# Narrower context columns in three projections, and the norm of each tile issued behind its own output projection

## The chip, the cores and the metric

One core of one Trainium2 chip runs the whole program. The time is device microseconds (us) of one execution; lower is better. Shapes are partitions x elements. PE is the matrix engine, DVE the vector engine, ACT the scalar engine, POOL the general engine, SP the queue that issues most DMAs. Each engine works through its own list of instructions in order; an instruction that waits holds up all that stand behind it on that engine.

## The reference, cut to what matters

Two layers of a block with three token mixers (a gated linear attention "ml", a decayed linear attention "hg", a differential softmax attention "da") and a gated feed-forward network. The input has 256 latent tokens `x` and 256 context tokens `ctx`; only `x` is returned.

```python
for l in range(DEPTH):                       # DEPTH = 2
    with_ctx = l < DEPTH - 1                 # the last layer makes no context output
    pc = split_cols(hc @ w_in + b_in)        # context rows: keys and values are needed in both layers,
    px = split_cols(hx @ w_in + b_in)        # queries only where with_ctx
    ...
    yx = jnp.concatenate([mx, gx, ax], axis=-1) @ w_out
    x = x + gx1 * rmsnorm(yx, g_post_mix[l])
    hx = rmsnorm(x, g_pre_ffn[l]) * (1.0 + ax2) + sx2
    x = x + gx2 * rmsnorm(swiglu(hx, ...), g_post_ffn[l])
```

So in the second layer the query columns of the context rows, and the gate columns of the context rows, are used by nothing.

## The kernel before

Tokens are four tiles of 128 rows: tiles 0 and 1 are context, 2 and 3 are latent. `full` is true in the first layer and false in the second; `qt` are the tiles that need queries (all four, then 2 and 3), `halves` the halves that need an output.

A projection is `gemm_tm`. It takes 256 columns of a weight at a time. Each weight block (512 rows x 256 columns) is loaded as `wraw`, cast by ACT to `whi` (L297), and the rest `wraw - whi` is made by DVE as `wlo` (L298), both in the format fp32r; there are two buffers of each. For every tile and each of the 8 slices of the contraction, PE loads a 128x128 piece of the activation `hT` as weights and streams 128x256 of `whi` or `wlo` past it: two products with `whi` (activation high and low part) and one with `wlo`. All of them have line L302. One projection of one tile is thus 24 products of 256 columns, and of four tiles 96. A PSUM bank `mm` holds two tiles (0 and 1, or 2 and 3); `add_bias` (L913) or `ev_vo` (L1069, L1076) takes a bank out.

In the second layer the query, key and value columns of da and ml come in blocks of 256: `qk` (three blocks, q is 0 to 383, k is 384 to 767), then the rest of the da values, `ev_vo` (three blocks: 0 to 383 values, 384 to 767 gates), and `mqk` (three blocks, again q then k). Block 0 is made for tiles 2 and 3 alone. Block 1 straddles the border, and is made whole for all four tiles.

The order on every engine is made when the program is built: a scheduler places instructions by priority and by its own estimates of how long each takes, and uses the projections as filler between the dependent steps of the mixers. The two places of concern are these. While the last two heads of hg run in lockstep (`hg_mix`, L811 to L868, then `hg_out`, L880 to L886: ACT copies `Ck`, PE multiplies into `mx`, DVE updates `Kh` and `Qd`), PE is given the products of `qk` blocks 0 and 1 between those steps. While `da_tile` runs for tiles 2 and 3 (L982 scores, L984 maximum, L988 exponentials, L994 difference, L997 transposes, L999 copy, L1003 values), PE is given the products of `ev_vo` and the first of `mqk`. Behind each of these two blocks come stretches of projections alone: behind hg the rest up to the transposes of `pad` (L968) that open da, behind da the rest up to the transposes of `mqk` (L1100).

At the end of the mixers `out_rest` makes the output projection. In the second layer the last half of its columns is made tile by tile (tile 2, then tile 3), and behind each tile `ev_z` (L1175 product with the gate, L1177 squares) and `post_norm` (L471, L473 on POOL, L475 into `R`) are issued. After both, `norm_T` calls `norm_rows` for each tile (L426 squares of `R` on ACT, `rstd` L415 and L416 on POOL, L428 scaled rows `nsc` on DVE), then PE transposes `nsc` (L447, L455), and ACT and DVE make `hT` for the feed-forward network (L461 to L466).

Of the kernel before, what the change touches and what calls it, by code (L numbers as in the profile page):

```python
# [15 lines left out]
ALU = mybir.AluOpType  # L16
# [85 lines left out]
def dit_block(ctx: ExitStack, tc: tile.TileContext, x, c, ctx_in, c_ctx, w_ada, b_ada, g_pre_mix,  # L102
# [220 lines left out]

    def gemm_tm(srcs, act, tiles, evac, pre=None):

        n = sum(p.shape[-1] for p in srcs[0])
        tiles = list(tiles)
        wide = n > 256  # L330
        bank = lambda t: t if wide else t // 2
        banks = {b: pst([P, 512] if wide else [P, 2, 256], mm=True) for b in sorted({bank(t) for t in tiles})}
        dst = lambda t: banks[t][:, :n] if wide else banks[bank(t)][:, t % 2, :n]
        new = lambda t: wide or t - 1 not in tiles or t % 2 == 0
        for si, blk in enumerate(blocks_of(srcs)):
            end = si == len(srcs) - 1
            if pre is not None and end:
                pre()
            if wide and end:
                for t in tiles:  # L340
                    upper(dst(t), blk, act, t, si == 0)
                    lower(dst(t), blk, act, t, True)
                    evac([t], dst(t))
            else:

                for t in tiles:
                    upper(dst(t), blk, act, t, si == 0 and new(t))
                for t in tiles:
                    lower(dst(t), blk, act, t, end)
            ada_step()  # L350
        if not wide:
            for tb, b in banks.items():
                tt = [t for t in tiles if bank(t) == tb]
                evac(tt, b[:, tt[0] % 2:tt[-1] % 2 + 1, :n])
# [254 lines left out]
    for l in range(DEPTH):  # L609
# [301 lines left out]

        def add_bias(dst, w, nb, bb):
            return lambda tt, ps: V.tensor_tensor(dst[:, tt[0]:tt[-1] + 1, w:w + nb], ps[:, :, :nb],  # L913
                                                  bb.over(0, nb, len(tt)), op=ALU.add)

        qk = stg.tile([P, 4, 768], F32, tag="qk", name=nm("qk"))
        for i in range(3):
            bb = Bias([b_in[l, O_DAQ + i * 256:O_DAQ + (i + 1) * 256]])
            gemm_tm(w_src(w_in[l], O_DAQ + i * 256, 256), hact, qt if i == 0 else range(4), add_bias(qk, i * 256, 256, bb), pre=bb.load)
        bb = Bias([b_in[l, O_DAV:O_DAV + 256]])  # L920
# [138 lines left out]
        for i in range(3):  # L1059
            bb = Bias([b_in[l, O_MLV + i * 256:O_MLV + (i + 1) * 256]])  # L1060

            def ev_vo(tt, ps, i=i, bb=bb):
                c_ = 0
                while c_ < 256:
# [13 lines left out]
                    c_ += w  # L1078
            gemm_tm(w_src(w_in[l], O_MLV + i * 256, 256), hact, range(4) if i < 2 else qt, ev_vo, pre=bb.load)
        mqk = stg.tile([P, 4, 768], F32, tag="qk", name=nm("mqk"))  # L1080
        for i in range(3):
            bb = Bias([b_in[l, O_MLQ + i * 256:O_MLQ + (i + 1) * 256]])
            gemm_tm(w_src(w_in[l], O_MLQ + i * 256, 256), hact, qt if i == 0 else range(4), add_bias(mqk, i * 256, 256, bb), pre=bb.load)

# [75 lines left out]

        Z, zss = {}, {}

        zbank = {}
# [28 lines left out]
        def out_rest(hf):  # L1192
# [6 lines left out]
            for cb in range(4):  # L1199
                hi, lo = ws[cb] = wload([w_out[l, 0:512, cb * 256:(cb + 1) * 256]])  # L1200
                if full or cb < 2:
                    for t in tt_:
                        out_mm(t, cb, hi, 0, True, False, False)
                    for t in tt_:
                        out_mm(t, cb, lo, 0, False, False, True)
                        if cb % 2:
                            ev_z(t, cb // 2)
            if not full:

                for t in tt_:  # L1210
# [3 lines left out]
                    with tc.high_priority(offset=CHAIN):  # L1214
                        ev_z(t, 1)
                        post_norm(t, Z[t], zss[t])

        ada_flush()
# [33 lines left out]
        with tc.tile_pool(name=f"ff{l}", bufs=1, reuse_waits="tile") as ff:  # L1252
# [5 lines left out]
            for hf in halves:  # L1258
                scr = norm_scr(ff, "nsc")
                if full:  # L1260
# [3 lines left out]
                else:  # L1264
                    with tc.high_priority(offset=CHAIN):
                        norm_T(u1, s1_, hf, scr)
            Z = {t: yp.tile([P, D], F32, tag=f"Y{t}", name=nm("Z")) for t in qt}
# [107 lines left out]
```

## Time and profile before

| what | us |
|---|---|
| median of 3 runs (lowest, highest) | 1347.56 (1346.56, 1349.05) |
| profiled execution, its own time | 1347.59 |
| its span (first to last instruction on the trace) | 1345.9 |
| PE busy in it | 1284.2 (95%) |
| DVE, ACT, POOL busy | 898.6, 624.9, 202.3 |

The second layer starts at about 815 us of the span, its hg mixer ends near 976, da runs from 999 to 1058, the output projection ends at 1139 and the feed-forward network fills 1151 to 1335. A row of the timeline is: start us, duration us, engine, line, operation, result<-inputs, shapes, count, and in brackets the idle time ahead of it with what ended that. Several instructions of a kind in a row are one row; its duration runs to the end of the last. The duration of a matrix product includes its drain, so the spacing of products, and not their duration, tells what a stream of them costs.

### The profile page before, as it was taken

To read this page: it belongs to the slowest core of one execution; us is meant where nothing else is said; L and a number is where in the kernel's file an instruction comes from. 1 tells how busy PE (TensorE), PEld (TensorE's weight loads), DVE (VectorE), ACT (ScalarE), POOL (GpSimd) and SP (SyncE) were. 2 spreads that over 40 slices of the span, in tenths; PEclk is the share of its full clock that TensorE was granted. 3 is DMA by queue.
4 is the path that set the end of the run, shared out by engine and by line. 5 is a ranking of instruction groups with operands and counts; after the bars stand their busy time and mean duration, and the time that the engine had idled before them with its cause. 6 is when DMAs were issued, how large, how long until landed. Compare 5 with 4: busy or idle time off the path is not lost.

```text
span 1345.9 us, 23128 instructions
## 1 busy us (share of the span) xinstructions
PE 1284.2 (95%) x9022; PEld 1094.6 (81%) x9022; DVE 898.6 (67%) x1564; ACT 624.9 (46%) x1188; POOL 202.3 (15%) x304
## 2 busy tenths in 40 slices
PE   7998999999989899999999999899999998999997
PEld 5785889778888798778887888778897998788886
DVE  4899998554688998476336348566855456666666
ACT  3436352578354653212221236546536724554543
POOL 3133202111142300001000003133111202000001
PEclk9999999999989999999999999899999999899999
DMA  9772526132244677477335235532331313456563
GB/s 290 227 221 75 164 64 201 41 114 72 95 141 142 192 253 229 141 255 243 116 100 178 94 111 151 148 95 63 104 95 51 122 47 109 142 188 188 188 188 125
DMA packets 158443, 194.05 MB, mean 144 GB/s; under 512 B 10524, under 2 KB 132806, under 8 KB 158334
## 3 DMA queue, kind: packets, MB, share of 16 engines
q1 hardware_dynamic: 156910, 188.89, 44.9%
q0 software_dynamic: 1424, 3.68, 1.0%
q8 instruction: 71, 1.16, 0.3%
q14 instruction: 38, 0.31, 0.1%
HBM read 191.47 MB, written 1.08 MB: 143 GB/s over the span
## 4 chain that ended last, share of the span: by engine, by line
PE 76%; DVE 10%; ACT 5%; issue 4%; DMA 3%; POOL 3%; SPq 0%; DVEq 0%; POOLq 0%; ACTq 0%
PE mm L302 62%; DMA araw<-in_w_ada_dram 2%; PE mx L1126 2%; DVE wlo L298 2%; PE mx L982 2%; PE mx L1003 1%; DVE acc L228 1%; PE mm L1114 1%; ACT whi L297 1%; POOL rstd L416 1%; PE mx L997 1%; PE mm L164 1%; DVE accq L228 1%; PE mx L880 1%; PE ada L233 1%
## 5 line engine op out<-in xcount | busy, mean ns | idle before, releaser
L297 ACT CAST whi<-wraw 128x1024 fp32r<-128x1024 f32 (+1 forms) x247 | 256.4, 1039 | 415.7 <-PE mm L302 365.2
L298 DVE TENSOR_TENSOR wlo<-wraw,whi 128x1024 fp32r<-128x1024 f32 (+1 forms) x243 | 295.8, 1218 | 193.0 <-PE mm L302 94.4
L302 PE MATMUL mm<-hT,whi 128*128 128x512 f32 (+1 forms) x1568 | 352.0, 372 | 4.4 <-ACT hT L465 2.1
L302 PEld LDWEIGHTS mm<-hT,whi 128*128 128x128 f32 x1568 | 270.8, 189 | 55.7 <-issue 4.0
L302 PE MATMUL mm<-whi,hT 128*128 128x256 f32 (+1 forms) x1792 | 264.3, 293 | 3.1 <-ACT hT L1157 1.4
L302 PEld LDWEIGHTS mm<-whi,hT 128*128 128x128 f32 x1792 | 234.0, 192 | 19.2 <-issue 8.4
L302 PE MATMUL mm<-hT,wlo 128*128 128x256 f32 (+1 forms) x960 | 185.0, 334 | 0.0
L302 PEld LDWEIGHTS mm<-hT,wlo 128*128 128x128 f32 x960 | 152.9, 190 | 21.1 <-issue 0.4
L302 PE MATMUL mm<-wlo,hT 128*128 128x256 f32 (+1 forms) x896 | 140.8, 292 | 0.0
L302 PE MATMUL mm<-whi,GT 128*128 128x512 f32 x504 | 129.5, 397 | 0.0
L302 PEld LDWEIGHTS mm<-wlo,hT 128*128 128x128 f32 x896 | 119.1, 191 | 10.9 <-issue 10.4
L302 PEld LDWEIGHTS mm<-whi,GT 128*128 128x128 f32 x504 | 93.7, 188 | 24.5 <-ACT whi L297 1.6
L228 DVE SCALAR_TENSOR_TENSOR accq<-araw,csil,accq 128x1024 f32<-128x1024 f32 x63 | 81.2, 1295 | 29.8 <-DMA araw<-in_w_ada_dram 29.7
L302 PE MATMUL mm<-wlo,GT 128*128 128x512 f32 x252 | 70.0, 396 | 0.0
L228 DVE SCALAR_TENSOR_TENSOR acc<-araw,csil,acc 128x1024 f32<-128x1024 f32 x49 | 62.8, 1306 | 4.6 <-DMA araw<-in_w_ada_dram 4.4
L302 PEld LDWEIGHTS mm<-wlo,GT 128*128 128x128 f32 x252 | 47.3, 188 | 11.3
L415 POOL TENSOR_SCALAR rstd<-hss 128x1 f32<-128x1 f32 (+2 forms) x44 | 18.8, 427 | 241.7 <-ACT hsq L656 159.9
L1327 POOL TENSOR_TENSOR Z<-Z,gg 128x512 f32<-128x512 f32 x6 | 9.4, 1572 | 234.1 <-ACT sqz L1326 234.1
L988 ACT ACTIVATE e<-mx,damx 128x512 f32<-128x512 f32 (+1 forms) x48 | 29.3, 618 | 26.3 <-DVE damx L985 26.3
L811 ACT COPY Ck<-Kh 128x512 f32<-128x512 f32 (+1 forms) x56 | 28.8, 525 | 25.7 <-DVE Kh L836 18.9
L416 POOL TENSOR_TENSOR rstd<-rstd,mhalf 128x1 f32<-128x1 f32 (+2 forms) x58 | 40.0, 690 | 4.7
L984 DVE TENSOR_REDUCE damx<-mx 128x1 f32<-128x512 f32 (+1 forms) x48 | 28.3, 598 | 18.0 <-PE mx L982 17.1
(283 smaller groups left out, 1499.9 us busy)
## 6 DMA issues: line engine op xcount, KB each, us to landing
araw<-in_w_ada_dram SPq DMA_DIRECT2D x80, 512.0 KB
wraw<-in_w_in_dram SPq DMA_DIRECT2D x68, 512.0 KB
wraw<-in_w_ffn_down_dram SPq DMA_DIRECT2D x50, 512.0 KB
wraw<-in_w_ffn_gate_dram SPq DMA_DIRECT2D x48, 512.0 KB
wraw<-in_w_ffn_up_dram SPq DMA_DIRECT2D x48, 512.0 KB
wraw<-in_w_out_dram SPq DMA_DIRECT2D x24, 512.0 KB
aw<-in_w_ada_dram SPq DMA_DIRECT2D x16, 512.0 KB
wraw<-in_w_in_dram SPq DMA_DIRECT2D x12, 256.0 KB
```

Source lines behind the costliest of these rows:

```text
L164: PE.matmul(acc0[3][:, :P], lhsT=ident, rhs=ident, start=True, stop=True, skip_group_check=True)
L228: V.scalar_tensor_tensor(out=a, in0=raw, scalar=csil[:, k, r:r + 1], in1=a, op0=ALU.mult, op1=ALU.add)
L297: S.copy(hi[:, :nk, :n], raw[:, :nk, :n])
L298: (eng or V).tensor_tensor(lo[:, :nk, :n], raw[:, :nk, :n], hi[:, :nk, :n], op=ALU.subtract)
L302: PE.matmul(ps, lhsT=lhs, rhs=rhs, start=first, stop=last, skip_group_check=True)
L415: G.tensor_scalar(o[:, :width], ss, 1.0 / n, EPS, ALU.mult, ALU.add)
L416: G.tensor_tensor(o[:, :width], o[:, :width], mhalf[:, :width], op=ALU.pow)
L811: S.copy(C[:, q0:].rearrange("p (a b i) -> p b a i", b=2, i=m), vap(K_, 2 * m * pq0, [[512 + m, 2], [2 * m, np_], [1, m]]))
L982: PE.matmul(pv[j], lhsT=qkT[0][64 * j:64 * j + DA_D, h, t * P:(t + 1) * P], rhs=qkT[1][64 * j:64 * j + DA_D, h, :nk], start=True, stop=True)
L984: V.reduce_max(mx[:, j:j + 1], pv[j], axis=AX.X)
L988: S.activation(e[:, j, :nk], pv[j], AF.Exp, bias=mx[:, 2 + j:3 + j], scale=sc, accum_out=mx[:, 4 + j:5 + j])
L1126: PE.matmul(po[:, i, d_, :], lhsT=W[d_, s_][0][:, t * P - W[d_, s_][2]:(t + 1) * P - W[d_, s_][2]], rhs=Vml[:, s_, h, :], start=n_ == 0, s ...
```

## The change

Two edits, both in effect in the second layer alone.

First, `gemm_tm` takes `ctx_cols`, and for tiles 0 and 1 it multiplies only those columns. It is given for block 1 of `qk`, of `ev_vo` and of `mqk`, where 128 of the 256 columns are wanted. The number of products stays as it is; 48 in each of the three blocks, 144 in all, have 128 columns in place of 256. The two `add_bias` evacuations are narrowed alike.

Second, `norm_rows` of a tile is issued right behind its own `post_norm` in `out_rest`, with its scratch tile allocated ahead of that, and `norm_T` is handed the rows.

```diff
-    def gemm_tm(srcs, act, tiles, evac, pre=None):
+    def gemm_tm(srcs, act, tiles, evac, pre=None, ctx_cols=None):
...
+        part = lambda t: slice(*ctx_cols) if ctx_cols and t < 2 else slice(0, n)
...
+            of = lambda t: (blk[0][:, :, part(t)], blk[1][:, :, part(t)], blk[2])
...
-                    upper(dst(t), blk, act, t, si == 0 and new(t))
+                    upper(dst(t)[:, part(t)], of(t), act, t, si == 0 and new(t))
                 for t in tiles:
-                    lower(dst(t), blk, act, t, end)
+                    lower(dst(t)[:, part(t)], of(t), act, t, end)
...
+        need = lambda i, a, b: (a, b) if i == 1 and not full else None
...
+                a, b = cc_ if cc_ and tt[0] < 2 else (0, nb)
+                V.tensor_tensor(dst[:, tt[0]:tt[-1] + 1, w + a:w + b], ps[:, :, a:b], bb.over(a, b, len(tt)), op=ALU.add)
...
+            gemm_tm(w_src(w_in[l], O_DAQ + i * 256, 256), hact, qt if i == 0 else range(4), add_bias(qk, i * 256, 256, bb, need(i, 128, 256)),
+                    pre=bb.load, ctx_cols=need(i, 128, 256))
...
-            gemm_tm(w_src(w_in[l], O_MLV + i * 256, 256), hact, range(4) if i < 2 else qt, ev_vo, pre=bb.load)
+            gemm_tm(w_src(w_in[l], O_MLV + i * 256, 256), hact, range(4) if i < 2 else qt, ev_vo, pre=bb.load, ctx_cols=need(i, 0, 128))
...
+            gemm_tm(w_src(w_in[l], O_MLQ + i * 256, 256), hact, qt if i == 0 else range(4), add_bias(mqk, i * 256, 256, bb, need(i, 128, 256)),
+                    pre=bb.load, ctx_cols=need(i, 128, 256))
...
             if not full:
+                nscr.append(norm_scr(ff, "nsc"))
+                scr1 = nscr[0]
...
                         post_norm(t, Z[t], zss[t])
+                        xrows.append(norm_rows(t, scr1[0][:, t - 2]))
...
-                        norm_T(u1, s1_, hf, scr)
+                        norm_T(u1, s1_, hf, scr, xrows)
```

The built order changes with it at three places. In the names, `mm_` are projection banks and `mx_` the mixers' banks; a trailing 128x256 or 128x128 is the result's shape and x16 a count.

PE, behind the last products of `hg_out` (`mx_9719`) in the second layer: `mm_9840` and `mm_9841` are block 1 of `qk` for tiles 0, 1 and tiles 2, 3; `mm_9954` is block 2. Before:

```order
L302 MATMUL mm_9841<-wlo_9898,hT 128x256 x4
L886 MATMUL mx_9734<-ident,oT_9732 128x128 x2
L302 MATMUL mm_9841<-wlo_9898,hT 128x256
L302 MATMUL mm_9954<-whi_9957,hT 128x256 x16
L302 MATMUL mm_9955<-whi_9957,hT 128x256 x16
```

With the change:

```order
L302 MATMUL mm_9840<-whi_9897,hT 128x128 x3
L888 MATMUL mx_9734<-ident,oT_9732 128x128 x2
L302 MATMUL mm_9841<-whi_9897,hT 128x256 x16
L302 MATMUL mm_9840<-wlo_9898,hT 128x128 x8
L302 MATMUL mm_9841<-wlo_9898,hT 128x256 x8
L302 MATMUL mm_9954<-whi_9957,hT 128x256 x16
L302 MATMUL mm_9955<-whi_9957,hT 128x256 x16
```

Five products of block 1 stood behind the hg steps, and 35 stand there now; from `mm_9954` to the transposes of `pad` both lists go on alike, with 192 products.

PE, at the last head of da (`mx_10547` its last scores, `mx_10559` and `mx_10569` the transposes of tiles 2 and 3, `mx_10588` and `mx_10602` their products with the values; `mm_10758`, `mm_10759` are block 1 of `ev_vo`, `mm_10878` its block 2, `mm_10946` block 0 of `mqk`). Before:

```order
L982 MATMUL mx_10547<-qkT_10201,qkT_10200 128x512
L302 MATMUL mm_10758<-wlo_10816,hT 128x256 x3
L302 MATMUL mm_10759<-wlo_10816,hT 128x256 x8
L302 MATMUL mm_10878<-whi_10880,hT 128x256 x16
L302 MATMUL mm_10878<-wlo_10881,hT 128x256 x2
L997 MATMUL mx_10559<-ident,e_10542 128x128 x4
L302 MATMUL mm_10878<-wlo_10881,hT 128x256 x6
L302 MATMUL mm_10878<-whi_10910,hT 128x256 x2
L997 MATMUL mx_10569<-ident,e_10553 128x128 x4
L1024 MATMUL mx_10576<-Mp_8336,ident_610 128x256
L1003 MATMUL mx_10588<-Vda_8329,aT_10564 128x96 x4
L302 MATMUL mm_10878<-whi_10910,hT 128x256 x9
```

With the change:

```order
L990 MATMUL mx_10547<-qkT_10201,qkT_10200 128x512
L302 MATMUL mm_10759<-whi_10815,hT 128x256 x7
L1005 MATMUL mx_10559<-ident,e_10542 128x128 x4
L302 MATMUL mm_10759<-whi_10815,hT 128x256 x9
L302 MATMUL mm_10758<-wlo_10816,hT 128x128 x8
L302 MATMUL mm_10759<-wlo_10816,hT 128x256 x8
L302 MATMUL mm_10878<-whi_10880,hT 128x256 x6
L1005 MATMUL mx_10569<-ident,e_10553 128x128 x4
L1032 MATMUL mx_10576<-Mp_8336,ident_610 128x256
L1011 MATMUL mx_10588<-Vda_8329,aT_10564 128x96 x4
L1011 MATMUL mx_10602<-Vda_8329,aT_10574 128x96 x4
L302 MATMUL mm_10878<-whi_10880,hT 128x256 x5
```

By `mx_10602` the list before has used up block 1 and three eighths of block 2's second half; the new one is an eighth into block 2. Behind `mx_10602`, up to the transposes of `mqk`, stood 253 products of 256 columns; now 234 of 256 and 48 of 128 stand there.

DVE, at the end of the output projection (`Z_11657`, `R_4236` are tile 2, `Z_11659`, `R_4238` tile 3; `wlo_11865` and `wlo_11887` belong to the feed-forward network; `nsc` are the normed rows). Before:

```order
L475 SCALAR_TENSOR_TENSOR R_4236<-Z_11657,rstd_11768,R_4236 128x1024
L1175 TENSOR_TENSOR Z_11659<-mm_11510,gg_11631 128x512
L298 TENSOR_TENSOR wlo_11865<-wraw_11863,whi_11864 128x1024
L471 TENSOR_SCALAR zss_11660,ss_11798<-zss_11660 128x2
L298 TENSOR_TENSOR wlo_11887<-wraw_11885,whi_11886 128x1024
L475 SCALAR_TENSOR_TENSOR R_4238<-Z_11659,rstd_11800,R_4238 128x1024
L428 TENSOR_SCALAR nsc_11806<-R_4236,rstd_11809 128x1024
L428 TENSOR_SCALAR nsc_11806<-R_4238,rstd_11815 128x1024
```

With the change:

```order
L477 SCALAR_TENSOR_TENSOR R_4236<-Z_11657,rstd_11769,R_4236 128x1024
L1185 TENSOR_TENSOR Z_11659<-mm_11510,gg_11631 128x512
L298 TENSOR_TENSOR wlo_11865<-wraw_11863,whi_11864 128x1024
L298 TENSOR_TENSOR wlo_11887<-wraw_11885,whi_11886 128x1024
L430 TENSOR_SCALAR nsc_11739<-R_4236,rstd_11774 128x1024
L473 TENSOR_SCALAR zss_11660,ss_11805<-zss_11660 128x2
L477 SCALAR_TENSOR_TENSOR R_4238<-Z_11659,rstd_11807,R_4238 128x1024
L430 TENSOR_SCALAR nsc_11739<-R_4238,rstd_11812 128x1024
```

The scaled rows of tile 2 moved ahead of the sums `zss` and the residual `R` of tile 3. On ACT the squares of tile 2's `R` moved ahead of tile 3's L1177, and on POOL the two steps of tile 2's `rstd` ahead of tile 3's L473.

## Rows read from the trace of the kernel before

**Rows 1.** The page: busy time of each engine, and the chain that ended last.

```profile
PE 1284.2 (95%) x9022; PEld 1094.6 (81%) x9022; DVE 898.6 (67%) x1564; ACT 624.9 (46%) x1188; POOL 202.3 (15%) x304
PE 76%; DVE 10%; ACT 5%; issue 4%; DMA 3%; POOL 3%; SPq 0%; DVEq 0%; POOLq 0%; ACTq 0%
```

**Rows 2.** By stretch: from:to, length, busy PE, PEld, DVE, ACT, POOL, clock, DMA share.

```profile
948.00:960.00 12.00, 11.43 (x182) 10.04 (x180) 12.00 (x28) 5.69 (x13) 3.97 (x2) 1.00 0.42 130
960.00:969.50 9.50, 9.24 (x123) 8.26 (x122) 7.89 (x23) 7.18 (x25) 0.00 (x0) 1.00 0.19 57
975.90:998.90 23.00, 23.00 (x194) 23.00 (x194) 10.83 (x21) 6.05 (x7) 5.79 (x11) 1.00 0.40 110
1021.60:1058.40 36.80, 35.65 (x234) 28.02 (x233) 22.63 (x54) 24.88 (x63) 6.00 (x18) 1.00 0.19 54
1058.40:1089.10 30.70, 30.70 (x258) 30.70 (x258) 11.27 (x14) 14.62 (x30) 6.02 (x11) 1.00 0.45 143
1138.90:1150.70 11.80, 4.22 (x17) 3.00 (x16) 8.29 (x13) 5.60 (x11) 4.73 (x6) 0.63 0.43 133
```

**Rows 3.** Timeline of PE: streams of products of several widths, second layer.

```profile
967.87 0.61 PE L855 MATMUL mx<-Qd,Kh 128*128 128x128 f32 x4
...
1071.79 4.00 PE L302 MATMUL mm<-whi,hT 128*128 128x256 f32 x32
1075.63 2.08 PE L302 MATMUL mm<-wlo,hT 128*128 128x256 f32 x16
...
1104.88 5.50 PE L1126 MATMUL mx<-Vml,Dt 128*128 128x97 f32 x48
1110.16 0.48 PE L302 MATMUL mm<-whi,hT 128*128 128x256 f32 x2
...
1200.51 2.03 PE L302 MATMUL mm<-whi,GT 128*128 128x512 f32 x8
1202.38 1.10 PE L302 MATMUL mm<-wlo,GT 128*128 128x512 f32 x4
```

**Rows 4.** Timeline of DVE: its waits at the end of the hg block.

```profile
961.34 1.23 DVE L298 TENSOR_TENSOR wlo<-wraw,whi 128x1024 fp32r<-128x1024 f32 x1 [0.58 <-PE mm L302]
...
968.52 0.29 DVE L858 TENSOR_SCALAR Qd<-Qd,T 128x128 f32<-128x128 f32 x1 [0.73 <-PE mx L855]
```

**Rows 5.** Timelines of ACT, DVE and PE: the last head of da.

```profile
1048.71 1.03 ACT L297 CAST whi<-wraw 128x1024 fp32r<-128x1024 f32 x1
...
1052.72 0.75 DVE L994 SCALAR_TENSOR_TENSOR e<-e,damx 128x512 f32<-128x512 f32 x1
...
1053.61 0.63 PE L997 MATMUL mx<-ident,e 128*128 128x128 f32 x4
...
1055.03 0.60 PE L997 MATMUL mx<-ident,e 128*128 128x128 f32 x4
...
1057.55 1.03 PE L1003 MATMUL mx<-Vda,aT 128*128 128x96 f32 x8
```

**Rows 6.** Timeline of all engines: the norm between output projection and feed-forward network.

```profile
1137.86 0.56 POOL L473 TENSOR_TENSOR rstd<-ss,mhalf 128x1 f32<-128x1 f32 x1 [18.39 <-DVE zss L471]
1138.45 1.28 DVE L475 SCALAR_TENSOR_TENSOR R<-Z,rstd,R 128x1024 f32<-128x1024 f32 x1 [0.67 <-POOL rstd L473]
...
1140.63 0.63 POOL L481 DMA_DIRECT2D gg<-gd  x1 [2.22 <-DVE Z L1175]
...
1141.46 1.22 DVE L298 TENSOR_TENSOR wlo<-wraw,whi 128x1024 fp32r<-128x1024 f32 x1
1141.63 1.48 POOL L473 TENSOR_TENSOR rstd<-ss,mhalf 128x1 f32<-128x1 f32 x1 [0.37 <-DVE zss L471]
...
1143.14 1.28 DVE L475 SCALAR_TENSOR_TENSOR R<-Z,rstd,R 128x1024 f32<-128x1024 f32 x1 [0.47 <-POOL rstd L473]
...
1144.46 1.06 ACT L426 ACTIVATE nsc<-R 128x1024 f32<-128x1024 f32 x1 [2.31 <-DVE R L475]
...
1145.15 0.76 DVE L428 TENSOR_SCALAR nsc<-R,rstd 128x1024 f32<-128x1024 f32 x1 [0.72 <-POOL rstd L416]
```

More of the change, by code (lines that the diff above doesn't have):

```diff
@@ L909, in dit_block, with add_bias, ev @@
         hst.close()
-        def add_bias(dst, w, nb, bb):
-            return lambda tt, ps: V.tensor_tensor(dst[:, tt[0]:tt[-1] + 1, w:w + nb], ps[:, :, :nb],
-                                                  bb.over(0, nb, len(tt)), op=ALU.add)
+        need = lambda i, a, b: (a, b) if i == 1 and not full else None
+        def add_bias(dst, w, nb, bb, cc_=None):
+            def ev(tt, ps):
+                a, b = cc_ if cc_ and tt[0] < 2 else (0, nb)
+                V.tensor_tensor(dst[:, tt[0]:tt[-1] + 1, w + a:w + b], ps[:, :, a:b], bb.over(a, b, len(tt)), op=ALU.add)
+            return ev
         qk = stg.tile([P, 4, 768], F32, tag="qk", name=nm("qk"))
@@ L918, in dit_block @@
             bb = Bias([b_in[l, O_DAQ + i * 256:O_DAQ + (i + 1) * 256]])
-            gemm_tm(w_src(w_in[l], O_DAQ + i * 256, 256), hact, qt if i == 0 else range(4), add_bias(qk, i * 256, 256, bb), pre=bb.load)
+            gemm_tm(w_src(w_in[l], O_DAQ + i * 256, 256), hact, qt if i == 0 else range(4), add_bias(qk, i * 256, 256, bb, need(i, 128, 256)),
+                    pre=bb.load, ctx_cols=need(i, 128, 256))
         bb = Bias([b_in[l, O_DAV:O_DAV + 256]])
@@ L1082, in dit_block @@
             bb = Bias([b_in[l, O_MLQ + i * 256:O_MLQ + (i + 1) * 256]])
-            gemm_tm(w_src(w_in[l], O_MLQ + i * 256, 256), hact, qt if i == 0 else range(4), add_bias(mqk, i * 256, 256, bb), pre=bb.load)
+            gemm_tm(w_src(w_in[l], O_MLQ + i * 256, 256), hact, qt if i == 0 else range(4), add_bias(mqk, i * 256, 256, bb, need(i, 128, 256)),
+                    pre=bb.load, ctx_cols=need(i, 128, 256))
         dst_.close()
@@ L1161, in dit_block @@
         Z, zss = {}, {}
+        xrows, nscr = [], []
         zbank = {}
@@ L1258, in dit_block @@
             for hf in halves:
-                scr = norm_scr(ff, "nsc")
+                scr = norm_scr(ff, "nsc") if full else nscr[0]
                 if full:
```

## The prediction

> **What bounds the kernel now.** I read the page first. PE is busy for 95% of the span, and 76% of the chain that ended last is PE [rows 1]. So work taken from PE should be time, where PE is what is waited for. Whether it is must be asked for each stretch that the change touches, so the second view is busy time by stretch [rows 2]. In the hg block (948 to 969.5) PE is nearly full, but DVE has 12.00 of 12.0 us to 960 and 7.89 of 9.5 behind that: PE is full because the planner had projections at hand to fill it, and DVE paces the block. From 975.9 to 998.9 and from 1058.4 to 1089.1 there are projections alone, and PE is busy for the whole of it; there each product more or less is time. In the da block (1021.6 to 1058.4) PE is full again with filler, while a chain from scores to maximum, exponentials, transposes and values runs through all engines. From 1138.9 to 1150.7 PE is idle for two thirds, and a chain over ACT, POOL and DVE decides.
>
> **The price of a product.** Streams of 256 columns take 3.84 us for 32 (starts 1071.79 and 1075.63 [rows 3]), 0.120 us each. 144 of them shrink to 128 columns; the trace has no fp32r product so narrow. The nearest rows are L1126: it too loads 128 weight columns for each record, streams 97 columns, and 48 of its records take 5.28 us (1104.88 to 1110.16), 0.110 each. I read this as the weight load setting the pace once the stream is short, and take 0.110: a narrow product saves 0.010 us, all 144 of them 1.4 us. The lower bound is the stream alone: 512 columns cost 1.87/8 = 0.234 (1200.51 to 1202.38), so 256 columns fewer save 0.114, and 128 fewer 0.057: 0.063 us. The upper bound is what a plain f32 product of 128 columns does at L855: the four records in its row are two products, so two records each, 0.22 us at 0.110.
>
> [...] No row here with 128 weight columns comes below 0.110, so I stay with the row.
>
> **The move behind the hg block.** The saving is small, but the planner has also moved filler. Between the last `mx_9719` and the transposes of `pad` stood 4 + 1 + 192 = 197 products of 256 columns, 197 x 0.120 = 23.64 us. Now 3 + 8 = 11 narrow and 16 + 8 + 192 = 216 wide ones stand there: 25.92 + 1.21 = 27.13 us. This stretch gets 3.5 us longer, since PE is its bound [rows 2]. The block ahead of it has so much less to do on PE, and could end earlier only as far as DVE lets it. Up to 960 DVE never rests, so PE would just wait there. Behind 960 DVE rests for 1.6 us in all; two rows hold most of it [rows 4]. The 0.58 us ahead of `wlo` is a wait for a projection; in the new order this `wlo` stands further back, behind another level of DVE work, and still waits for projections that now come later. The 0.73 us at L858 is a wait for a product that itself waits for `Kh` and `Qd` from DVE. I take 0.5 us of the 1.6 as won (from 0 to 1.1). Net +3.0 us.
>
> **The move behind da.** Behind `mx_10602` stood 253 products of 256 columns, 30.36 us; now 234 wide and 48 narrow ones, 28.08 + 5.28 = 33.36 us: +3.0 us, with the narrow ones of `mqk` counted. What does the da block give back? At the last head the difference `e` ran at 1052.72, late because ACT made a cast (1048.71, 1.03 us) between its two exponentials and DVE a `wlo` and bias adds ahead of it [rows 5]. The new order puts these behind, so tile 2's transposes can come about 3.2 us earlier than 1053.61. But then ACT has the copy of the transposes, an exponential, the same cast and an exponential to do before tile 3's difference, some 3.2 us, and tile 3's transposes land at about 1055.3, no earlier than now (1055.03). Only their copy gains, since ACT has no table load ahead of it any more; I put the last values product 0.8 us earlier than 1057.55 (0 to 1.5). Net +2.2 us.
>
> **The norm.** Tile 2's rows gain, but tile 3's decide, for `hT` needs both. `R` of tile 2 ends at 1139.73 (1138.45 + 1.28), its squares on ACT by 1140.9 (they take 1.16 with their sum, as from 1144.46). POOL is free of its DMA issue at 1141.26. The two steps of `rstd` then fall beside the two `wlo` of the feed-forward network on DVE, the second from 1141.46 to 1142.68. L473 shows what that does: 0.56 us alone at 1137.86, but 1.48 at 1141.63, ending just behind that `wlo` [rows 6]. So tile 2's `rstd` is there at 1143.1 to 1143.4, and `nsc` (0.76) ends at about 1144.0. Until then DVE holds tile 3's `zss`, which stands behind `nsc` in its list; it was done by 1141.6 before. Then come `zss` 0.2, L473 0.56, and `R` of tile 3 at about 1144.8 instead of 1143.14. All that follows is as before: +1.7 us (1.1 if POOL were not held up, 1.9 if both steps were). Tile 3's own L1177 squares, 0.5 us later on ACT, hide behind this; so do tile 2's transposes, which PE now makes in its idle time.
>
> [...]
>
> The clock stood at half speed for part of this stretch (0.63 on average [rows 2]); PE idles there for about as long as before, and I count no change, but 1 us either way for when it comes back. The narrower `add_bias` saves DVE some tenths where nobody waits for it. The first layer's order does not change.
>
> **Sum.** 3.0 + 2.2 + 1.7 = +6.9 us. The profiled execution took 1347.59 us, the median of the runs is 1347.56: 1354.5 us. By the ends of its own terms this case covers 1352.3 to 1357.
>
> **Rivals.** *Two records.* If a product of 128 columns is run as L855 is, at 0.22 us, the stretch behind hg has 25.92 + 2.42 = 28.34 us (+4.7), the block wins nothing; behind da 28.08 + 10.56 = 38.64 (+8.3), of which the block gives 0.5 back; with the norm +14.2, 1361.8 us. For it: the plain f32 products of this width do that. Against: every fp32r product of the trace, 256 to 512 columns, is one record.
>
> *Stream alone.* At 0.063 us the two stretches grow by 3.0 and 0.7; less 0.5 and 0.8, plus 1.7: +4.1, 1351.7 us. Against it stand the rows of L1126.
>
> *The blocks shrink with their filler.* If PE's full queue, and not DVE or the chain, paces both blocks, each ends as much earlier as it lost filler, and only the total counts: -1.4 from the 144 products, +1.7 for the norm, 1347.9 us, not slower. Its price is the 5.2 us of the two moves; it decides once the blocks win more than 3.9 us together, where I gave them 1.3. For it: in da many steps follow directly on filler. Against: DVE's 12.00 of 12 us. With the stream's price besides, it would be 144 x 0.057 = 8.2 less and 1.7 more, 1341.1: faster.
>
> *The norm does as it is meant,* and tile 3 loses nothing: 1352.8, within the first case's reach.
>
> **How the numbers follow.** Two kernels can be told apart here from about 0.2%, 2.7 us. Forecast 0.55, two records 0.25, stream alone 0.06: 0.86 slower. Shrinking blocks 0.11: same. With the stream's price 0.03: faster. The range runs from 1350.0, below the stream's case, to 1362.5, over the case of two records; it leaves out the shrinking blocks and the tails, some 0.17.
>
> **What would show it.** Spacing of the 128-column products of L302: 0.110 us (0.063 or two records of 0.110 for the rivals). Behind the hg block, the start of the `pad` transposes some 3 us later than 998.9; the end of the last values product to the start of the `mqk` transposes 3 us longer; PE waiting for ACT's `Ck` and for `e` in the blocks. In the norm, `R` of tile 3 starting about 6.3 us behind `R` of tile 2, where it was 4.69 (1138.45 to 1143.14). Wrong would be: blocks that end 3 us earlier, or a `rstd` of tile 2 that is not held up.

## The result, and the profile after

The changed kernel takes 1365.38 us (median of 4 runs, 1364.13 to 1368.42) where the kernel before takes 1347.06 in the same comparison: 1.0138 times as long, 95% interval 1.0117 to 1.0159. It is slower, as forecast, but by 18.3 us and not by 6.9, and it lies above the range. The profiled run is the longest of the four, 1368.42 us, with a span of 1366.7.

The page after, busy time of each engine, answers to [rows 1]:

```profile
PE 1300.8 (95%) x9022; PEld 1109.3 (81%) x9022; DVE 899.2 (66%) x1564; ACT 622.4 (46%) x1186; POOL 197.8 (14%) x304
```

PE has as many instructions as before, 144 of them are narrower, and yet it is busy for 16.6 us longer. The next rows show why: its granted clock, which the profile gives as a share of full speed, is lower (0.970 over the profiled run, 0.985 before). The same stretches as in [rows 2], moved to where they lie now (from:to, length, busy PE, PEld, DVE, ACT, POOL, clock, DMA share):

```profile
947.30:959.30 12.00, 10.20 (x165) 8.79 (x164) 12.00 (x28) 5.24 (x13) 3.94 (x2) 0.90 0.43 129
959.30:972.50 13.20, 11.23 (x113) 9.91 (x112) 9.59 (x32) 7.15 (x25) 0.00 (x0) 0.76 0.14 41
978.90:1005.50 26.60, 26.60 (x224) 26.60 (x224) 11.26 (x22) 6.99 (x8) 5.80 (x11) 1.00 0.35 96
1028.20:1075.60 47.40, 45.19 (x205) 35.43 (x204) 21.65 (x53) 22.54 (x63) 5.84 (x19) 0.68 0.09 26
1075.60:1109.30 33.70, 33.70 (x286) 33.70 (x286) 12.20 (x15) 14.61 (x28) 4.71 (x11) 1.00 0.48 152
1159.10:1172.30 13.20, 4.26 (x17) 3.00 (x16) 8.34 (x13) 5.64 (x11) 3.53 (x6) 0.60 0.38 119
```

The column to read is the clock. It was 1.00 in both blocks before; now it is 0.90 and 0.76 in the hg block and 0.68 in the da block. The da block lasts 47.4 us in place of 36.8, with fewer records on PE (205 for 234) that are busy for 9.5 us more. In shorter windows (same columns) the clock of its middle is 0.50:

```profile
1040.00:1045.00 5.00, 4.00 (x22) 2.48 (x22) 2.60 (x6) 1.99 (x8) 1.68 (x5) 1.00 0.00 0
1045.00:1050.00 5.00, 5.00 (x21) 4.15 (x21) 1.81 (x5) 4.60 (x12) 0.59 (x2) 0.57 0.00 0
1050.00:1055.00 5.00, 4.66 (x23) 4.50 (x23) 2.27 (x4) 0.74 (x2) 0.00 (x0) 0.50 0.34 105
1055.00:1060.00 5.00, 5.00 (x18) 3.33 (x17) 0.38 (x2) 2.71 (x10) 1.90 (x6) 0.50 0.01 2
1060.00:1065.00 5.00, 5.00 (x10) 2.21 (x9) 3.36 (x8) 1.45 (x4) 0.08 (x1) 0.50 0.01 3
```

On the timeline of PE (start, duration, what ran, idle time ahead in brackets) the waits for ACT and DVE that the prediction named are there, and behind them the steps of the block itself run slowly:

```profile
964.39 0.33 PE L822 MATMUL mx<-Qd,Ck 128*32 128x32 f32 x16 [1.44 <-ACT Ck L813]
...
1040.76 1.98 PE L990 MATMUL mx<-qkT,qkT 48*128 48x512 f32 x6
...
1044.82 1.22 PE L990 MATMUL mx<-qkT,qkT 48*128 48x512 f32 x2 [1.00 <-ACT e L996]
...
1054.06 3.57 PE L1011 MATMUL mx<-Vda,aT 128*128 128x96 f32 x16
...
1060.47 2.07 PE L990 MATMUL mx<-qkT,qkT 48*128 48x512 f32 x2
...
1063.51 2.07 PE L990 MATMUL mx<-qkT,qkT 48*128 48x512 f32 x2
...
1073.26 0.63 PE L1005 MATMUL mx<-ident,e 128*128 128x128 f32 x4 [0.73 <-DVE e L1002]
...
1073.85 1.92 PE L1011 MATMUL mx<-Vda,aT 128*128 128x96 f32 x16
```

The first of those rows is in the hg block, the others are in da. Before, the row that answers to 1044.82 was this:

```profile
1037.16 1.12 PE L982 MATMUL mx<-qkT,qkT 48*128 48x512 f32 x2 [0.97 <-ACT e L988]
```

Two scores take 2.07 us at a clock of 0.50 (1060.47) where they took 1.12 at 1.00, sixteen products with the values 3.57 at 1054.06 (0.50) and 1.92 at 1073.85, when the clock is back at 1.00. These steps are the chain of the block, so their time is the block's time. The wait for `e` is not new: it is 1.00 us now and was 0.97, at a clock of 1.00.

Where the time went, by steps of the two profiled runs (each stretch's length after less its length before; the ends are products on PE: hg from the first product of one `hg_out` with the values to that of the next, 928.07 to 973.03 before, da from its first scores to what follows its last product with the values, 1008.57 to 1058.36; the windows above differ in length by the same amounts, within 0.1 us):

| stretch | predicted | measured |
|---|---|---|
| hg block | -0.5 | +3.7 |
| behind hg, to the `pad` transposes | +3.5 | +3.65 |
| da block | -0.8 | +10.6 |
| behind da, to the `mqk` transposes | +3.0 | +3.03 |
| norm, to the first product of the feed-forward network | +1.7 | +1.35 |

The rest is -1.5 us in parts that the change doesn't touch. The three sums of products and of the norm hold; the two blocks miss by 4.2 and 11.4 us.

### The profile page after: what moved, and what is told of

It reads as the page before. It is cut to its first block, busy times and chain, and to the rows that moved or that the text cites. A ratio compares the mean times of both kernels' runs of the same rounds, so it can differ in the third digit from the quotient of the medians.

```text
span 1366.7 us, 23130 instructions
## 1 busy us (share of the span) xinstructions
PE 1300.8 (95%) x9022; PEld 1109.3 (81%) x9022; DVE 899.2 (66%) x1564; ACT 622.4 (46%) x1186; POOL 197.8 (14%) x304
## 4 chain that ended last, share of the span: by engine, by line
PE 78%; DVE 9%; ACT 5%; issue 4%; POOL 3%; DMA 1%; SPq 0%; POOLq 0%; DVEq 0%; ACTq 0%
PE mm L302 63%; PE mx L990 2%; PE mx L1135 2%; DVE wlo L298 2%; PE mx L1011 1%; POOL rstd L418 1%; PE mx L1005 1%; PE mm L1123 1%; ACT whi L297 1%; PE mx L882 1%; PE ada L233 1%; PE mm L164 1%; DVE acc L228 1%; DVE Qd L841 1%; PE mx L857 1%
## 5 line engine op out<-in xcount | busy, mean ns | idle before, releaser
L302 PE MATMUL mm<-whi,hT 128*128 128x256 f32 (+2 forms) x1792 | 271.5, 298 | 3.0 <-ACT hT L1166 1.4
L302 PEld LDWEIGHTS mm<-whi,hT 128*128 128x128 f32 x1792 | 240.6, 198 | 23.2 <-issue 12.5
L302 PE MATMUL mm<-wlo,hT 128*128 128x256 f32 (+2 forms) x896 | 140.3, 293 | 0.0
L418 POOL TENSOR_TENSOR rstd<-rstd,mhalf 128x1 f32<-128x1 f32 (+2 forms) x58 | 42.4, 731 | 4.7
L990 PE MATMUL mx<-qkT,qkT 48*128 48x512 f32 (+1 forms) x96 | 38.1, 607 | 3.9 <-ACT e L996 3.6
```

What stands on the lines that cost most here:

```text
L302: PE.matmul(ps, lhsT=lhs, rhs=rhs, start=first, stop=last, skip_group_check=True)
L418: G.tensor_tensor(o[:, :width], o[:, :width], mhalf[:, :width], op=ALU.pow)
L990: PE.matmul(pv[j], lhsT=qkT[0][64 * j:64 * j + DA_D, h, t * P:(t + 1) * P], rhs=qkT[1][64 * j:64 * j + DA_D, h, :nk], start=True, stop=True)
```

## The experiments

The theory: with less filler (projections placed between the steps of a chain) PE has less to do in the blocks, its granted clock falls, and the chain runs through the slow products. The rivals: the new order itself lengthens the chains, and the clock only marks that; or one edit spoils the other.

**More work for PE, in the same order.** This kernel has the changed kernel's list of instructions on every engine, word for word. Only 96 narrow products take the slower format.

```diff
-            gemm_tm(w_src(w_in[l], O_MLV + i * 256, 256), ..., ctx_cols=need(i, 0, 128))
+            gemm_tm(w_src(w_in[l], O_MLV + i * 256, 256), ..., ctx_cols=need(i, 0, 128) and need(i, 0, 128) + (1,))
...  # likewise for qk; mm() casts operands of a marked product:
-        PE.matmul(ps, lhsT=lhs, rhs=rhs, start=first, stop=last, skip_group_check=True)
+        lhs, rhs = (a.bitcast(F32) if plain[0] and ps.shape[-1] == 128 else a for a in (lhs, rhs)); PE.matmul(ps, lhsT=lhs, rhs=rhs, start=first, stop=last, skip_group_check=True)
```

> The changed kernel with one edit: the 96 narrow products of qk and of ev_vo, those that lie in or right behind the hg and the da block, are multiplied as plain f32 in place of fp32r, two records of some 0.11 us each in place of one. Nothing else is changed, and every engine has the same list of instructions as the changed kernel. So PE gets 96 x 0.11 = 10.6 us more work, 85 of the products in the two blocks (37 + 48), 11 behind hg. Theory (the changed kernel lost 14.3 us in the two blocks because PE idled there and its granted clock fell to 0.5): with PE kept busy the clock stays at 1.00 from 930 to 1070 us, the hg block is about 3.7 us shorter than in the changed kernel, the da block 9 to 10.5 us shorter, the stretch behind hg 1.2 us longer: 1365.4 - 12.2 = 1353, from 1351 to 1356. Rival (the new order itself, its later wlo and bias adds, makes the chains of the blocks longer, and the clock is only a mark of waiting): no block gets shorter, 1365.4 to 1376.

Measured: 1358.32 us (ratio to before 1.0083, 1.0069 to 1.0097), 7.1 us less than the changed kernel with some 10.6 us more for PE to do (an estimate, 96 x 0.11). Its hg block in two windows, its stretch behind hg, and its da block:

```profile
948.80:960.80 12.00, 11.49 (x193) 9.99 (x195) 12.00 (x28) 5.21 (x13) 3.96 (x2) 1.00 0.45 137
960.80:971.00 10.20, 9.56 (x127) 8.66 (x128) 8.01 (x24) 6.81 (x24) 0.00 (x0) 1.00 0.19 53
977.40:1005.10 27.70, 27.70 (x235) 27.70 (x233) 11.27 (x22) 7.09 (x8) 5.79 (x11) 1.00 0.33 92
1027.80:1066.00 38.20, 36.94 (x252) 29.50 (x252) 21.77 (x53) 22.03 (x63) 5.85 (x18) 1.00 0.12 32
```

The clock is 1.00 throughout. PE has 96 records more than in the changed kernel (9118 for 9022) and is busy for 7.6 us less (1293.2 for 1300.8). The da block is 9.1 us shorter than in the changed kernel (steps +1.4 and +10.6 over before), the hg block 2.95 (+0.74 and +3.69), and the stretch behind hg 1.05 longer, all three near what the theory gave. The rival of order alone falls: it allowed no shorter block. Order is not quite without effect, though: of the 14.3 us that the blocks lost, 12.1 are gone here and 2.2 stay at a clock of 1.00 (0.74 + 1.43), from later steps or from the added work of this kernel, which were not told apart. The total missed the theory's 1351 to 1356, by its own arithmetic: it took the block losses of the changed kernel's longest run from the median of its runs, which is 3.0 us lower, and the parts ahead of hg and behind the norm were 2.0 us longer in this profile than in the changed kernel's, where the edit touches nothing.

**The two edits apart.** The first kernel has only the norm edit, the second only the narrow columns.

```diff
# norm_only
-            gemm_tm(w_src(w_in[l], O_MLV + i * 256, 256), ..., ctx_cols=need(i, 0, 128))
+            gemm_tm(w_src(w_in[l], O_MLV + i * 256, 256), ..., ctx_cols=None)
...                                              # likewise for qk and mqk, and in their add_bias
# cols_only
-                        xrows.append(norm_rows(t, scr1[0][:, t - 2]))
...
-                        norm_T(u1, s1_, hf, scr, xrows)
+                        norm_T(u1, s1_, hf, scr)
```

> Only the second edit: squares and normed rows behind each tile's own part of the output projection, all columns of the context tiles multiplied as before. The order in the hg and da blocks is that of the kernel before. Theory: the blocks and their clock stay as before (1.00), and the norm alone costs 1.4 us: 1348.5, from 1348.0 to 1349.2, R of tile 3 starts 6.1 us behind R of tile 2. Rival (the norm moves more than its stretch, through what is placed ahead of it): over 1350.

Measured: 1348.67 us, ratio 1.0013 (1.0004 to 1.0022); the step over the norm is +1.35, and `R` of tile 3 starts 6.11 us behind `R` of tile 2.

> Only the first edit: the narrow context columns in qk, ev_vo and mqk, the norm as before. Theory: the whole loss of the two blocks (3.7 + 10.6) and of the stretches behind them (3.6 + 3.0) is here: 1365.4 - 1.4 = 1364.0, from 1362.5 to 1365.5, with the clock at 0.5 for some 30 us of the da block. Rival (the two edits make each other worse): under 1360.

Measured: 1362.85 us, ratio 1.0119 (1.009 to 1.0148). So nearly all of the loss is here, and the edits add up as far as the spread lets one say (15.8 + 1.6 = 17.4 of 18.3 us). But its four runs reach from 1358.52 to 1368.17, and the profiled one is the shortest. Its da block (same columns) stood at a clock of 0.96, not the 30 us at 0.5 that the theory expected:

```profile
1027.90:1066.90 39.00, 34.09 (x207) 25.89 (x204) 21.93 (x54) 22.41 (x64) 6.06 (x19) 0.96 0.12 32
```

Here one sees what the slow clock hides. On the same list of da instructions PE is busy for 34.1 us of 39.0 and waits for 4.9; in the changed kernel it is busy for 45.2 of 47.4 and seems to wait for only 2.2, because the slow products fill the time. By steps this da block is 1.8 us longer than before and the changed kernel's 10.6, with the same list of instructions on PE: the 8.7 us between them go with the clock. The two runs also show that idle time by itself does not settle the clock: with 4.9 us of waits it stayed at 0.96. How far the clock falls differs from run to run of one program (its mean lies between 0.971 and 0.984 in the four runs here).

**One block at a time.**

```diff
# cols_qk: ctx_cols in qk alone; cols_vo: in ev_vo alone; the norm of before in both
-            gemm_tm(w_src(w_in[l], O_MLV + i * 256, 256), ..., ctx_cols=need(i, 0, 128))
+            gemm_tm(w_src(w_in[l], O_MLV + i * 256, 256), ..., ctx_cols=None)
```

> The kernel before with narrow context columns in block 1 of qk alone. The order in and behind the hg block is that of the changed kernel (37 narrow products in the block, 19 + 216 wide and 11 narrow ones moved as there), in da that of before. Theory: the hg block gets 2.2 to 3.7 us longer, since PE idles and its clock falls for part of it, the stretch behind it 3.65; the da block stays at 36.8 us (1021.6 to 1058.4 before) with its clock at 1.00: 1347.05 + 6.5 = 1353.5, from 1352.5 to 1354.8. Rival (the da block of the changed kernel is slow because of what happened in hg): the da block is longer here too, over 1358.

Measured: 1355.52 us, ratio 1.0067 (1.0052 to 1.0083), 0.7 us above the range given. By steps the hg block is +3.6, the stretch behind it +3.65, the da block -0.1 at its old clock of 1.00: no carry-over from hg to da.

> The kernel before with narrow context columns in block 1 of ev_vo alone; hg is that of before. Behind da stand 282 products of 256 columns in place of 253. Theory: the stretch behind da gets 29 x 0.120 = 3.5 us longer, the da block 1.8 to 10.6 us, as far as the clock falls in the run: between 1352.4 and 1361, with a wider spread than other kernels, and the longer the lower the granted clock. Rival (the order alone, no clock): 1350.6 in every run, spread within 2 us.

Measured: 1355.30 us, ratio 1.0075 (1.0049 to 1.0102). In the profile the da block is +4.5 with a clock of 0.88 over it, the stretch behind da +3.4. The runs lie as wide apart as forecast, the lowest and the highest just outside the range; the rival of order alone allowed 2 us. The single runs, with the mean granted clock of each, beside those of cols_only, of the changed kernel and of f32_blocks, whose blocks run full:

| kernel | runs: us (clock) |
|---|---|
| cols_vo | 1350.36 (0.988), 1354.12 (0.984), 1355.30 (0.983), 1360.88 (0.974), 1361.40 (0.976) |
| cols_only | 1358.52 (0.984), 1360.05 (0.980), 1365.65 (0.975), 1368.17 (0.971) |
| changed kernel | 1364.13 (0.975), 1364.92 (0.974), 1365.85 (0.973), 1368.42 (0.970) |
| f32_blocks | 1357.10 (0.985), 1358.23 (0.985), 1358.41 (0.985), 1359.40 (0.986) |

The order of instructions of a row is the same in each of its runs; in the first three rows the time goes closely with the clock. The fastest run of cols_vo lies 4.0 us over the median of before in the same comparison (1346.39; its runs reach from 1343.59 to 1348.89), and 3.4 is what the products moved behind da cost in the profiled run. So its da block can have lost little; that run has no trace, and this is not shown.

**The norm's two causes.** As norm_only, with tile 2's scaled rows issued behind tile 3's `zss`.

```diff
+        if late is not None:
+            late.append((xn, t, rs))
+            return xn
         V.tensor_scalar_mul(xn, R[t], rs)
...
                     with tc.high_priority(offset=CHAIN):
+                        for xn_, t, rs in late:
+                            V.tensor_scalar_mul(xn_, R[t], rs)
                         norm_T(u1, s1_, hf, scr, xrows)
```

> As norm_only, but the scaled rows nsc of tile 2 are issued on DVE behind zss of tile 3, squares and rstd as there. Theory: two thirds of the loss was rstd of tile 2 standing ahead of tile 3's on POOL, held up beside wlo, and the other part nsc ahead of zss on DVE. R of tile 3 starts 5.4 us behind R of tile 2 (4.69 before, about 6.1 in norm_only): 1347.05 + 0.6 = 1347.7, from 1347.2 to 1348.3. Rival (all of the loss is nsc ahead of zss): 4.7 us, 1347.0; rival (the place of nsc is of no account): 6.1 us, 1348.7.

Measured: 1347.75 us, ratio 1.0009 (1.0000 to 1.0017). The timelines of POOL and DVE in it:

```profile
1140.95 1.43 POOL L418 TENSOR_TENSOR rstd<-rstd,mhalf 128x1 f32<-128x1 f32 x1
1142.36 0.84 POOL L478 TENSOR_TENSOR rstd<-ss,mhalf 128x1 f32<-128x1 f32 x1
...
1137.80 1.28 DVE L480 SCALAR_TENSOR_TENSOR R<-Z,rstd,R 128x1024 f32<-128x1024 f32 x1 [0.67 <-POOL rstd L478]
...
1141.87 0.15 DVE L476 TENSOR_SCALAR_CACHE_REDUCE zss<-zss 128x2 f32<-128x2 f32 x1
1142.42 0.75 DVE L1283 TENSOR_SCALAR nsc<-R,rstd 128x1024 f32<-128x1024 f32 x1 [0.39 <-POOL rstd L418]
1143.24 1.28 DVE L480 SCALAR_TENSOR_TENSOR R<-Z,rstd,R 128x1024 f32<-128x1024 f32 x1
```

`R` of tile 3 starts 5.44 us behind `R` of tile 2 (4.69 before, 6.11 in norm_only): the step is +0.7. So about half of the loss was `nsc` ahead of `zss` on DVE, where the expectation gave it a third. For the other half two things are left: tile 2's `rstd` on POOL (L418), behind which tile 3's (L478) starts at once at 1142.36, and `zss` itself, which now stands behind both `wlo` and ends at 1142.02. These two were not told apart.

**The part that moves nothing.** Narrow columns in `mqk` alone, where no block loses filler.

> The kernel before with narrow context columns in block 1 of mqk alone. No block has less filler; 48 products behind da have 128 columns. Theory: the stretch from the last values product of da to the transposes of mqk is 48 x 0.010 = 0.5 us shorter and nothing else changes, 1346.5 to 1347. Rivals: with the stream's price 2.7 us shorter, with two records 4.8 us longer.

Measured, in one run: 1345.84 us; the stretch behind da is 0.40 us shorter, 0.0083 for each of the 48 products, and the two blocks and the stretch behind hg are as before, within 0.1 us. (The time by itself, 1.2 us under before, does not show it: as much lies ahead of hg, where the edit touches nothing.) Its products on the timeline of PE (a row here holds 16 narrow products and then 16 wide ones):

```profile
1064.83 3.87 PE L302 MATMUL mm<-whi,hT 128*128 128x128 f32 x32
1068.54 2.02 PE L302 MATMUL mm<-wlo,hT 128*128 128x128 f32 x16
...
1075.95 4.00 PE L302 MATMUL mm<-whi,hT 128*128 128x256 f32 x32
1079.79 2.08 PE L302 MATMUL mm<-wlo,hT 128*128 128x256 f32 x16
```

From 1064.83 to 1068.54 are 3.71 us; the 16 wide ones take 16 x 0.120 = 1.92, so a narrow one takes 1.79/16 = 0.112.

**Sparing the same columns without thinning the blocks.** The second layer takes blocks of 384 columns (256 rows of the weight in each), so none straddles q and k, and context tiles skip whole products. The evacuations, by tile, are adapted.

```diff
+    def w_src4(w, c0, n):
+        return [[w[kh * 256:(kh + 1) * 256, c0:c0 + n]] for kh in range(4)]
...
+        else:                                   # not full; for mqk, and alike for ev_vo (wide_vm) and qk
+            for i in range(2):
+                bb = Bias2(O_MLQ + i * 384)
+                gemm_tm(w_src4(w_in[l], O_MLQ + i * 384, 384), hact, qt if i == 0 else range(4), add_bias_w(mqk, i * 384, bb), pre=bb.load)
...
# wide_kq: in qk, keys ahead of queries
-            for i in range(2):
+            for i in (1, 0):
```

> The kernel before, with the same columns spared in another way: in the second layer ev_vo and mqk take two blocks of 384 columns in place of three of 256, so that no block straddles the border and the context tiles skip whole products. A weight block then holds 256 rows. 480 products of 256 columns become 288 of 384; at 384/512 of the 0.234 us that 512 columns take, 0.176 us, that is 57.6 - 50.7 = 6.9 us less PE work. In the built order the da block has 169 of the wide products where 174 of 256 stood, 29.7 us of filler in place of 20.9. Theory (a saving pays if PE has as much at hand in the blocks as the planner meant): the clock stays at 1.00 in da, and the kernel gains 4 to 7 us: 1341.5, from 1339.5 to 1344. Rival (any saving of filler in these sections makes PE idle in da, and the clock falls): 1347 or more.

Measured: 1338.01 us, ratio 0.9932 (0.9916 to 0.9948). The da block is 7.6 us longer, with its clock at 1.00, the stretch behind it 16.7 us shorter; the time is 1.5 us under the range given. 24 products in a row take 4.16 us there, 0.173 each, a little less than the 0.176 assumed.

> As wide_vm, and qk in two blocks of 384 columns too. That takes another 240 x 0.120 - 144 x 0.176 = 3.5 us of work from PE. But in the built order it is taken from the hg block, whose last steps have no filler at all (projections placed between the two hg_out: 25.0 us, as in the changed kernel, where the kernel before has 28.9); behind hg stand 24.3 us in place of 23.6. Theory: the hg block gets 0.7 to 3.7 us longer in place of shorter, 1339 to 1342.5, no better than wide_vm's 1338.0 and more likely worse. Rival (PE work is time): 1334.5.

Measured: 1339.02 us, ratio 0.9944 (0.9930 to 0.9958), at the low end of the range given and no better than wide_vm though PE has less to do. The hg block is +3.15 with clocks of 0.86 and 0.80 in the two windows.

> As wide_all, but qk takes its key block (four tiles) ahead of its query block (tiles 2 and 3), so that projections are at hand up to the end of the hg block: 28.4 us of them lie between the two hg_out (28.9 in the kernel before, 25.0 in wide_all), and behind hg stand 20.9 us in place of 23.6. Theory (filler is to be spared behind a block, not in it): the hg block keeps its length and its clock of 1.00, the stretch behind it is 2.7 us shorter, the rest as in wide_vm: 1338.0 - 2.7 = 1335.3, from 1334 to 1337. Rival (384 columns in this block cost its chain more than they spare): 1338 or more.

Measured: 1334.38 us, ratio 0.9902 (0.9885 to 0.9918), in the range given, the best of all and 12.7 us under the kernel before. The hg block in two windows, the stretch behind it, the da block and the stretch behind that, first of wide_all, then of wide_kq:

```profile
945.60:957.60 12.00, 10.44 (x134) 8.55 (x134) 10.47 (x21) 4.57 (x9) 3.60 (x2) 0.86 0.43 122
957.60:970.20 12.60, 9.70 (x118) 7.88 (x111) 11.18 (x40) 7.27 (x27) 0.00 (x0) 0.80 0.16 44
976.60:1000.90 24.30, 23.68 (x167) 23.39 (x166) 11.26 (x27) 7.18 (x9) 5.50 (x11) 1.00 0.41 104
1024.10:1068.50 44.40, 43.70 (x238) 34.87 (x237) 28.76 (x67) 32.22 (x79) 7.41 (x20) 1.00 0.37 104
1068.50:1082.50 14.00, 14.00 (x83) 13.97 (x83) 5.47 (x11) 6.19 (x19) 4.47 (x11) 1.00 0.49 147
```

```profile
948.30:960.30 12.00, 10.74 (x155) 8.64 (x155) 11.53 (x28) 4.78 (x12) 2.18 (x2) 1.00 0.20 54
960.30:969.80 9.50, 8.88 (x94) 7.72 (x91) 7.51 (x23) 6.51 (x23) 0.00 (x0) 1.00 0.27 81
976.10:996.80 20.70, 20.45 (x149) 20.13 (x148) 11.78 (x26) 7.99 (x10) 6.27 (x11) 1.00 0.60 156
1019.90:1064.40 44.50, 43.77 (x238) 34.92 (x237) 28.79 (x67) 32.27 (x79) 7.43 (x20) 1.00 0.34 104
1064.40:1078.40 14.00, 14.00 (x84) 13.95 (x84) 5.48 (x11) 6.20 (x18) 4.48 (x11) 1.00 0.48 148
```

The same products, with keys ahead of queries, reach the end of the hg block. The block is as long as before (step 0.0) at a clock of 1.00, and the spared work comes off behind it (-2.4).

## Why the prediction was right and wrong

**Price of a product: right.** 0.112 measured, 0.110 forecast. Each narrow product is one record (144 of them, as many records as before), so the rival of two records is out, and so is the stream's 0.063. That the weight load sets this price is the prediction's reading; no run varied it.

**The moves behind the blocks: right.** +3.65 and +3.03 for +3.5 and +3.0, in the changed kernel as in cols_only. Why the planner moved filler can be narrowed: it made the same lists when these products were plain f32, which take two records each (f32_blocks has 96 records more for its 96 products). So it seems to hold a narrow fp32r product for as dear as a plain f32 one, and to fill the gaps of the blocks by that. In the hg block 7 narrow products stand between two steps (952.82 in the changed kernel) where 14 wide ones stood (953.53 before). This is read from the lists; what the planner reckons with is not shown.

**What the blocks give back: this is the step that failed.** For hg the prediction put "PE would just wait there" and -0.5 us, for da -0.8. Both terms have the wrong sign: +3.7 and +10.6. They asked how much earlier a block could end with less filler, and took an idle PE to cost nothing. But these blocks had a clock of 1.00 with filler in PE's gaps; with less of it the granted clock fell to 0.50 in parts of them (957 to 960, 968 to 973, 1048 to 1068), where the chain's own products took up to 1.9 times as long (3.57 us for 1.92). f32_blocks shows it: same lists, more work, clock 1.00, and 9.1 and 2.95 us less.

No single wait tells when the clock falls. The wait for `e` stands in f32_blocks too, at a clock of 1.00 (first row), and in the changed kernel the clock first fell in da at 1032, behind 12 us in which PE was busy for 11.8 (the last of them in the second row, the fall in the third):

```profile
1043.11 1.12 PE L990 MATMUL mx<-qkT,qkT 48*128 48x512 f32 x2 [1.00 <-ACT e L996]
```

```profile
1028.00:1032.00 4.00, 3.87 (x15) 1.58 (x12) 3.69 (x7) 2.38 (x7) 1.28 (x4) 1.00 0.01 4
1032.00:1036.00 4.00, 4.00 (x20) 4.00 (x20) 3.48 (x11) 1.81 (x5) 0.00 (x0) 0.51 0.49 145
```

As for the da chain at a clock that is nearly whole: the prediction saw tile 2's transposes of the last head 3.2 us earlier and tile 3's no earlier. In cols_only, counted from the last scores, they come 2.7 us earlier (2.01 us behind for 4.69) and 1.0 later (7.09 for 6.11). So there (0.96) da gains nothing either: the block is 1.8 us longer. The table load of 1.28 us that ACT had ahead of tile 3's copy (at 1055.05 before) comes behind the block in the changed kernel, at 1081.62, as foretold.

**The clock.** The prediction spoke of it for the norm alone, and counted "no change, but 1 us either way". There it holds: the stretch stood at 0.63 and now at 0.60, with 0.50 in parts of it (first before, then the changed kernel):

```profile
1146.00:1150.00 4.00, 3.70 (x15) 2.94 (x16) 1.77 (x4) 1.69 (x4) 0.55 (x1) 0.50 0.33 114
```

```profile
1166.00:1172.00 6.00, 2.81 (x11) 2.07 (x11) 2.27 (x5) 3.25 (x6) 0.74 (x2) 0.50 0.26 92
```

The same rows that showed a low clock where PE idles (0.63 in the last row of [rows 2], PE busy for 4.22 of 11.80 us) should have been put against the two blocks.

**The norm: right in kind, 0.35 us too dear.** +1.35 for +1.7, and tile 3's `R` at 6.11 us for 6.3. What the forecast rested on is there in the changed kernel (the first and the last row are `R` of tiles 2 and 3):

```profile
1158.69 1.28 DVE L477 SCALAR_TENSOR_TENSOR R<-Z,rstd,R 128x1024 f32<-128x1024 f32 x1 [0.67 <-POOL rstd L475]
...
1161.85 1.43 POOL L418 TENSOR_TENSOR rstd<-rstd,mhalf 128x1 f32<-128x1 f32 x1
...
1163.31 0.75 DVE L430 TENSOR_SCALAR nsc<-R,rstd 128x1024 f32<-128x1024 f32 x1 [0.47 <-POOL rstd L418]
1163.98 0.15 DVE L473 TENSOR_SCALAR_CACHE_REDUCE zss<-zss 128x2 f32<-128x2 f32 x1
...
1164.80 1.28 DVE L477 SCALAR_TENSOR_TENSOR R<-Z,rstd,R 128x1024 f32<-128x1024 f32 x1 [0.66 <-POOL rstd L475]
```

Tile 2's `rstd` takes 1.43 us beside `wlo`, as L473 took 1.48 in [rows 6]; tile 3's takes 0.55 at 1167.62, when DVE is idle. Tile 3's squares end at 1161.73, and `zss`, which stands behind `nsc` in DVE's list, starts at 1163.98. So the two tiles' steps follow as foretold. The forecast's 1.1, for a POOL that is not held up, is shown by no run: this step takes 1.43 us in norm_only and norm_split too.

**The sum.** With the five terms as forecast, +6.9; the three that stand come to +8.0 measured, and the blocks bring 14.3 in the profiled run, which is 3.0 us over the median; whether the blocks are shorter by that in the other runs is not shown. *The blocks shrink with their filler* was the rival furthest from the truth, since less filler made them longer. The range did not hold the time because no case in it let a block become longer. A small slip besides: by the ends of its own terms the forecast case reaches down to 1351.6, not 1352.3 (0.6 + 0.7 + 0.6 and 1 for the clock); nothing hangs on it.

**Still open:** why the clock falls further in one run of a program than in the next, and at what point of a block. The kernels with about as much filler in a block as before, or more, kept the clock of that block at 1.00 in the profiles (cols_qk, wide_vm and wide_kq in da, wide_vm and wide_kq in hg, where wide_kq has 28.4 us between the two `hg_out` for 28.9); those with less lost some of it (wide_all has 25.0 there). Where between these the clock begins to fall was not measured.

## What to carry to other kernels

Filler that is placed between the steps of a chain can also keep TensorE's clock up (1.00 in f32_blocks, 0.68 over the changed kernel's da block, with the same lists), so work spared there can cost more than it gives: look at the granted clock of the stretch, not at busy time, which rose as the clock fell (45.2 us in the changed kernel's da block, 36.9 in that of f32_blocks). Spare work where PE alone is the bound, and keep the blocks full (wide_kq and wide_all do the same products with two projections turned about, 4.6 us apart). Before narrowing products, drop whole ones: 128 of 256 columns spared 0.008 us a product, a product left out at 256 spares 0.120.

## What the runs showed of the hardware

The granted clock fell in stretches in which PE was still busy for most of the time: in cols_vo, 1035 to 1045, PE is busy for 8.3 of 10 us.

```profile
1030.00:1035.00 5.00, 4.47 (x27) 2.96 (x26) 2.23 (x6) 2.24 (x10) 2.15 (x6) 1.00 0.00 0
1035.00:1040.00 5.00, 3.94 (x20) 2.98 (x21) 2.18 (x6) 5.00 (x14) 0.58 (x2) 0.88 0.00 0
1040.00:1045.00 5.00, 4.36 (x30) 4.25 (x29) 2.27 (x4) 1.14 (x3) 0.00 (x0) 0.78 0.33 102
```

cols_vo spread over 11 us in five runs, and its time went with its clock; f32_blocks and wide_vm, whose blocks ran full, stayed within 2.3. Spread alone is no sign of it, though: cols_qk, whose hg block lost some of its clock (0.50 from 970 to 975), stayed within 0.7, and the kernel before reaches over 5.3 in 16 runs.

It can also go the other way. Behind the norm the feed-forward network starts at a clock of 0.50 (wide_vm, 1141 to 1145); in the profiles of wide_all and wide_kq the clock was back some 4 us sooner (1.00 from 1143 and from 1139), and the network took 2.1 us less than in the kernel before. First wide_vm, then wide_kq, the first 4 us of the network:

```profile
1141.00:1145.00 4.00, 3.74 (x10) 2.92 (x10) 3.25 (x6) 2.40 (x5) 0.00 (x0) 0.50 0.00 0
```

```profile
1139.00:1143.00 4.00, 3.28 (x20) 2.69 (x19) 3.54 (x7) 3.65 (x7) 0.00 (x0) 1.00 0.00 0
```

Of wide_kq's 12.7 us some 2 are of this kind in the profiled run; whether they hold in its other runs is not shown. Its forecast, made without them, stood 0.9 us above its median.
